# A buffer of its own for the first weight load of each block, paid for with two of four row buffers

## The chip, the cores and the metric

The kernel runs on one core of one Trainium2 chip. The metric is the device time of one execution in microseconds (us). The kernel before has a median of 1816.11 us over three runs (1810.0, 1816.11 and 1819.2).

## The reference

Two layers, each `x <- x + W_out(mixer(rms_norm(x)) * silu(gate))`, on a sequence of 1024 rows and a model width of 1024, with 16 heads of 64. Layer 1 is an attention over all earlier rows with a forget gate. Layer 2, which the change touches, has three groups of dilated windows:

```
qkv = proj[..., :3 * N_GROUPS * INNER].reshape(B, S, 3, N_GROUPS, N_HEADS, HEAD_DIM)
q = apply_partial_rotary(rms_norm(qkv[:, :, 0], q_g[:, None, :]), cos, sin)
k = apply_partial_rotary(rms_norm(qkv[:, :, 1], k_g[:, None, :]), cos, sin)
v = qkv[:, :, 2]
for g, (window, dilation) in enumerate(((128, 1), (512, 4), (2048, 16))):
    o_g, lse_g = dilated_window_attention(q[:, :, g], k[:, :, g], v[:, :, g], window, dilation)
wts = softmax(lses, axis=0)
o = sum over g of wts[g] * o_g
```

So layer 2 needs a projection with 9 x 1024 columns of weights, which is most of its work, then small attention tiles, a weighted sum over the groups, and the output projection.

## The kernel before, in words

**Blocks.** Layer 2 works through 24 blocks, in the list `order`: first group 0 of the eight head pairs, then for each head pair group 2 and group 1. A block projects the eight tiles of 128 rows (t = 0 to 7) by 384 columns of weights (keys, queries and values of two heads). One tile is 24 matmuls at line 313 of `project`: eight slabs of 128 weight rows, three products each, because every operand is split into a high and a low part. All three products of a slab go to one PSUM tile `pj`, of which there are three.

**Weights.** Class `Weights` brings the 384 columns of a block in four loads of two slabs each (`load`, the DMA at L253), into tiles `raw` of which there are two. For the value columns `bound` (L258, VectorE, "vm<-raw") takes a maximum, so a scale can be found later; `split` casts a slab to its high part on ScalarE (L289) and subtracts on GpSimd or, for slabs 4 and 6, on VectorE (L291). The split slabs go to tiles `w`, of which there are 12: eight that the running block multiplies with and four more. So slabs 0 to 3 of the next block can be split at any time in a block, and slabs 4 to 7 only when the last tile of the running block has used its first slabs. A `raw` tile is free again when `bound` and both splits of its two slabs are done.

**Order.** `Flow` counts slots, four to a tile and 32 to a block. `ahead` puts the steps for the next block at slots of the running one: loads at 0, 4, 13 and 20, bounds at 9, 14, 22 and 27, the scale at 28, splits at 10, 11, 15, 16, 29, 29, 30 and 30. These slots fix the order of the program. TensorE keeps that order (`manual_schedule`); for the other engines and for the one DMA queue, SyncE's (SP), the framework's planner makes the order in advance, from its own estimates of durations: what is ready, with a free buffer, goes when the engine is idle, the earlier in the program first. On the chip each engine and the queue then run that fixed order, and wait at the head of it.

**Head norms.** After every second tile `heads_pair` finishes the norms of two tiles: `u` at L378 reads the projection out of PSUM, and L422 scales it by a factor that lies in the same `pj` tile. Until L422 has run, that `pj` tile isn't free. A DMA transpose (L430, "qk_t<-hl") turns queries and keys; `dsw_pair` scores them (L450), and a second DMA transpose (L913, "ptt<-ph") turns the weights for the products with the values (L506 to L508).

**The tag `ga`.** In layer 2 tiles of 2 KB per partition with the tag `ga` are used in two places only. In block 7 (the last of group 0) `reload_x` brings the normed rows again in another column order: two loads per tile t (L983, "x<-xn_d", 16 in all), each followed by a cast on ScalarE (L987) and a subtraction on VectorE (L988) that write over columns of `xh` and `xl` when tile t has been projected. The next block needs these columns: its tile t = 3 reads the last of them. In block 23, the last, `turn_y` brings the finished attention rows of the first seven head pairs (L711, "yt<-y_d"), two loads per tile t of four and three column blocks, which TensorE turns at L346 ("pt<-ident,yt") for the output projection. For a pair of tiles the four loads are asked for at slots 0 to 3 after the second tile and the four turns stand at slots 4 to 7 in TensorE's order. Four tiles with the tag `ga` serve both places.

**Pools.** `lay` takes tiles from a pool of the running layer, with the number of buffers per tag from `CFG`; layer 2's numbers apply from the last tile of the first part of its gate projection on.

Of the kernel before, what the change touches and what calls it, by code (L numbers as in the profile page):

```python
# [51 lines left out]
def tile_cols(g, t):  # L52


    if g < 2:
        return slice(t * P, (t + 1) * P, 1)
    a = 2 * P * (t % 4) + t // 4
    return slice(a, a + 2 * 127 + 1, 2)
# [24 lines left out]
def trunk(ctx, tc, ins, out, cfg):  # L83
# [23 lines left out]
    layer = {}  # L107
# [8 lines left out]
    def lay(shape, dtype, name, tag):  # L116
        return layer["pool"].tile(shape, dtype, name=name, tag=tag, bufs=layer["bufs"][tag])
# [120 lines left out]
    class Weights:  # L238
# [7 lines left out]
                self.vm2 = sm.tile([P, KT // 2], F32R, name="vm2", tag="vm2")  # L246

        def load(self, i, tag=None):
            if tag is None:
                self.raw[i] = w_p.tile([P, 2, 384], F32, name="raw", tag="raw", bufs=2)  # L250
            else:
                self.raw[i] = lay([P, 2, 384], F32, name="raw", tag=tag)
            nc.sync.dma_start(self.raw[i][:, :, : self.n], self.src[:, 2 * i : 2 * i + 2, :])  # L253
# [54 lines left out]
    def project(w, cols):  # L308
        n = w.n
        ps = under["ps"] = ps_pj.tile([P, 512], F32, name="pj", tag="pj")  # L310
        for k in range(KT):
            for i, (a, j) in enumerate(((xh, 0), (xh, 1), (xl, 0))):
                nc.tensor.matmul(ps[:, :n], a[:, k, cols], w.slabs[k][:, j, :n], start=(k == 0 and i == 0), stop=(k == KT - 1 and i == 2))  # L313
            if k % 2:
                flow.tick()
        return ps
# [143 lines left out]
    def v_tile(vs):  # L460
        vt = lay([P, NT, 2, 129], F16, name="vt", tag="vt")
        nc.scalar.activation(vt[:, :, :, 128], vs.unsqueeze(2).broadcast_to([P, NT, 2]), AF.Copy)
        return vt
# [242 lines left out]
    def turn_y(t, g, slots):  # L706
        for h, (n, (s0, s1)) in enumerate(zip((4, 3), slots)):

            def load(h=h, n=n, s1=s1):
                yt = lay([P, 512], F32, name="yt", tag="ga")  # L710
                nc.sync.dma_start(yt[:, : n * P], y_d[tile_rows(g, t), 512 * h : 512 * h + n * P])  # L711

                def go():
                    transpose_rows(yt, 4 * h, n, t)
                    turned.add((t, h))

                flow.at(s1, go)

            flow.at(s0, load)
# [12 lines left out]
    for hp in range(NHP):  # L732
# [8 lines left out]
        vt = v_tile(w.vs)  # L741
        vsr = sm.tile([P, NT], F32, name="vsr", tag="vsr")
        nc.scalar.activation(vsr, rx[:, 0], AF.Copy, scale=w.vs)
        for t in range(NT):
            ps = project(w, tile_cols(0, t))
# [246 lines left out]
    for ci, (hp, g) in enumerate(order):  # L992
        w2 = (dsw_weights(ci + 1) if ci + 1 < len(order) else part(w_do, 0)).ahead()
        vt = v_tile(w.vs)
# [3 lines left out]
        for t in range(NT):  # L998
            if ci == NHP - 1:
                reload_x(t)  # L1000
            ps = project(w, tile_cols(g, t))
# [20 lines left out]
            else:  # L1022
                cmb = {}
# [31 lines left out]
    layer["cm"].__exit__(None, None, None)  # L1055


CFG = dict(pin=1, bc=((1, 0, 26), (1, 1, 28), (0, 0, 38), (0, 1, 46)), wl=(0x50, 0x50), ps=0, pv=100, ph_=100, ph=1, wbufs=12, pl=3, um=3, lpf=8, lsd=((16, 16), (16, 14), (14, 11)), ty2=((0, 4), (1, 5)), hb=1, ub=2, qb=1, nb=3, fox=(((0, 0, 2, 2), (2, 4)), ((0, 0), (4, 4))), due=(29, 33, 39, 45, 35, 41, 49, 57), l1=dict(ga=7, ptt=3, ph=2, p=4, qk_t=6, vt=3, gsl=3), l2=dict(ga=4, cmb=3, ptt=3, ph=2, p=2, qk_t=3, og=3, vt=3, gsl=3, par=1), wload=(0, 4, 13, 20), wbound=(9, 14, 22, 27), wscale=28, wsplit=(10, 11, 15, 16, 29, 29, 30, 30))


def host_layout(inputs):
# [49 lines left out]
```

## Time and profile before

| what | value |
|---|---|
| median of three runs | 1816.11 us |
| the profiled execution's own time | 1818.5 us |
| span of the trace in it | 1816.7 us |
| mean granted TensorE clock | 0.990 |
| busy: TensorE matmul, VectorE, ScalarE, GpSimd | 96%, 60%, 56%, 54% |

Times in a trace count from the first instruction. Busy is the share of the span in which an engine runs an instruction; matmuls overlap, so a busy TensorE is one that has no gap, not one at its peak. Layer 2's blocks lie from about 710 to 1720 us; block 7 from about 1036 to 1081, block 23 from about 1670 on. Then comes the output projection (L336) up to the end. A line of waits reads: engine and line that waited, what it waited for, us in total, times, longest.

### The profile page before, as it was taken

How to read it: one execution, taken by the hardware profiler on the slowest of the kernel's cores; microseconds unless marked ns; L12 is line 12 of the kernel's file. 1: busy time of each engine (PE TensorE's matmuls, PEld its weight loads, DVE VectorE, ACT ScalarE, POOL GpSimd, SP SyncE). 2: the span in 40 equal slices, each digit the busy share in tenths (PEclk: the TensorE clock that was granted, in tenths of full speed). 3: DMA queues.
4: the chain of work that ended last, by engine and by line, in shares of the span. 5: the costliest groups of instructions: out<-in, count | busy, mean ns of one | idle time of the engine just before them, and what ended most of it. 6: DMA issues, size and time to landing. Idle time of an engine off the chain costs nothing.

```text
span 1816.7 us, 38150 instructions
## 1 busy us (share of the span) xinstructions
PE 1737.0 (96%) x13276; PEld 1641.7 (90%) x13276; DVE 1093.3 (60%) x3674; ACT 1011.0 (56%) x2696; POOL 973.5 (54%) x1175
## 2 busy tenths in 40 slices
PE   7999999999988989999999999999999999999999
PEld 6999888888876779999999989999999999999877
DVE  8546666666664453365556585666675666667631
ACT  6536666666665465455555665555555555555620
POOL 4215565556545431255656566667576666757530
PEclk9999999999999999999999999999999999999999
DMA  8447999999999763456767687667677776667852
GB/s 285 127 130 140 193 190 185 176 177 183 187 190 207 213 188 114 127 113 134 142 133 144 146 191 143 157 140 152 138 163 144 162 151 143 149 140 179 189 154 85
DMA packets 653189, 290.79 MB, mean 160 GB/s; under 512 B 512306, under 2 KB 616754, under 8 KB 652996
## 3 DMA queue, kind: packets, MB, share of 16 engines
q1 hardware_dynamic: 652996, 288.36, 71.4%
q8 instruction: 104, 1.70, 0.4%
q14 instruction: 89, 0.73, 0.1%
HBM read 126.46 MB, written 37.03 MB: 90 GB/s over the span
## 4 chain that ended last, share of the span: by engine, by line
PE 45%; DMA 12%; DVE 6%; ACT 4%; issue 3%; POOL 3%; SPq 1%; DVEq 0%; POOLq 0%; ACTq 0%
PE pj L313 33%; PE pj L336 7%; DMA raw<-in_w_dsw 5%; PE s L450 2%; DMA qk_t<-hl 2%; DMA ptt<-ph 2%; DMA og_d<-og 1%; POOL hl L425 1%; POOL w L291 1%; DMA cmb<-og_d 1%; DVE w L291 1%; DVE hl L426 1%; DVE u L422 1%; PE ob L506 1%; DVE p L906 1%
## 5 line engine op out<-in xcount | busy, mean ns | idle before, releaser
L313 PE MATMUL pj<-w,xh 128*128 128x384 f32 (+2 forms) x4864 | 1259.6, 341 | 30.2 <-ACT w L289 7.3
L313 PEld LDWEIGHTS pj<-w,xh 128*128 128x128 f32 x4864 | 873.1, 191 | 38.9 <-DVE ge L481 7.8
L313 PE MATMUL pj<-w,xl 128*128 128x384 f32 (+2 forms) x2432 | 817.6, 336 | 0.2 <-DVE xl L530 0.2
L313 PEld LDWEIGHTS pj<-w,xl 128*128 128x128 f32 x2432 | 464.7, 191 | 0.9 <-DVE xl L530 0.9
L291 POOL TENSOR_TENSOR w<-raw,w 128x384 fp32r<-128x384 f32 (+2 forms) x258 | 261.7, 1035 | 233.3 <-ACT w L289 228.8
L498 POOL TENSOR_TENSOR ph<-p,ph 128x512 f16<-128x512 f32 (+3 forms) x176 | 172.9, 999 | 161.9 <-ACT ph L495 160.7
L289 ACT CAST w<-raw 128x384 fp32r<-128x384 f32 (+2 forms) x352 | 162.6, 501 | 114.8 <-PE pj L336 37.4
L425 POOL TENSOR_TENSOR hl<-u,hl 128x512 f16<-128x512 f32 x128 | 151.2, 1181 | 125.0 <-ACT hl L424 124.9
L912 POOL TENSOR_TENSOR ph<-p,ph 128x768 f16<-128x768 f32 (+2 forms) x96 | 155.3, 1618 | 102.9 <-ACT ph L911 102.9
L383 ACT ACTIVATE sq<-pj 128x256 f32<-128x256 f32 x256 | 97.2, 380 | 168.9 <-DVE u L378 167.2
L450 PE MATMUL s<-qk_t 128*128 128x128 f16 (+1 forms) x1504 | 162.0, 248 | 19.2 <-DVE acc L658 10.4
L336 PE MATMUL pj<-xh,w 128*128 128x512 f32 x512 | 170.4, 404 | 2.2 <-ACT p L907 1.1
L258 DVE TENSOR_REDUCE vm<-raw 128x1 f32<-128x256 f32 x128 | 53.6, 419 | 156.2 <-DMA raw<-in_w_dsw 118.6
L506 PEld LDWEIGHTS <-ptt 128*128 128x128 f16 x1136 | 102.9, 98 | 48.8 <-issue 27.5
L389 DVE SCALAR_TENSOR_TENSOR vt<-pj,vsr,vt 128x128 f16<-128x128 f32 x256 | 89.6, 350 | 93.2 <-ACT vt L388 92.8
L450 PEld LDWEIGHTS <-qk_t 128*128 128x128 f16 x1504 | 110.2, 98 | 36.1 <-issue 22.0
L424 ACT CAST hl<-u 128x512 f16<-128x512 f32 x128 | 79.2, 619 | 104.9 <-DVE u L422 88.6
L495 ACT CAST ph<-p 128x512 f16<-128x512 f32 (+3 forms) x176 | 88.9, 537 | 72.7 <-DMA ptt<-ph 72.3
L492 ACT ACTIVATE p<-p,acc 128x512 f32<-128x512 f32 (+2 forms) x192 | 109.0, 609 | 30.6 <-DVE acc L658 27.4
L336 PEld LDWEIGHTS pj<-xh,w 128*128 128x128 f32 x512 | 97.6, 191 | 24.5 <-DVE xr L779 1.5
L378 DVE TENSOR_TENSOR u<-pj,gr 128x256 f32<-128x256 f32 x256 | 106.4, 416 | 18.4 <-PE pj L313 18.3
L907 ACT ACTIVATE p<-p,og 128x128 f32<-128x128 f32 (+1 forms) x256 | 98.1, 441 | 33.6 <-DVE og L906 33.4
(171 smaller groups left out, 2609.4 us busy)
## 6 DMA issues: line engine op xcount, KB each, us to landing
raw<-in_w_dsw SPq DMA_DIRECT2D x96, 384.0 KB, 3.7
raw<-in_w_fox SPq DMA_DIRECT2D x32, 384.0 KB, 3.7
og_d<-og SPq DMA_DIRECT2D x64, 132.0 KB, 3.2
cmb<-og_d SPq DMA_DIRECT2D x64, 132.0 KB, 3.3
bc<-c_d SPq DMA_DIRECT2D x32, 256.0 KB, 3.9
gs_d<-ge SPq DMA_DIRECT2D x32, 192.0 KB, 3.2
xt<-in_xt SPq DMA_DIRECT2D x16, 256.0 KB, 6.1
xrow<-in_x SPq DMA_DIRECT2D x8, 512.0 KB, 6.3
```

The source lines that it names most:

```text
L289: nc.scalar.copy(w[:, 0, :n], raw[:, k % 2, :n])
L291: eng.tensor_sub(w[:, 1, :n], raw[:, k % 2, :n], w[:, 0, :n].bitcast(F32))
L313: nc.tensor.matmul(ps[:, :n], a[:, k, cols], w.slabs[k][:, j, :n], start=(k == 0 and i == 0), stop=(k == KT - 1 and i == 2))
L336: nc.tensor.matmul(ps[m], w.slabs[k][:, j, m * P : (m + 1) * P], a[:, k, 512 * b : 512 * (b + 1)], start=(k == 0 and x == 0), stop=(k == K ...
L378: nc.vector.tensor_mul(u[:, t % 2].rearrange("p (a b) d -> p a b d", a=2), ps[:, : 4 * HD].rearrange("p (a b d) -> p a b d", a=2, b=2), gr ...
L425: nc.gpsimd.tensor_sub(hl[:, :, :4, 1], u, hl[:, :, :4, 0])
L450: nc.tensor.matmul(s[:, c0 : c0 + cnt * P].rearrange("p (c s) -> p c s", c=cnt), qk[:, i, blk], kk[:, j : j + cnt, e], start=(h == 0), sto ...
L492: nc.scalar.activation(p, p, AF.Exp, bias=acc, scale=-1.0)
L498: (nc.gpsimd if pool_l else nc.vector).tensor_sub(ph[:, e, 1, cols], p, ph[:, e, 0, cols])
L506: nc.tensor.matmul(o[:, e, :], hi, vt[:, j, e, HD:], start=(b == 0), stop=False, skip_group_check=True)
L907: nc.scalar.activation(p[:, e], p[:, e], AF.Exp, bias=acc[:, e : e + 1], scale=-1.0)
L912: nc.gpsimd.tensor_sub(ph[:, 1], st["p"], ph[:, 0])
```

## The change

The first load of each set of weights, whenever layer 2's buffer numbers hold, goes to a tile with the new tag `raw0` (one buffer of 3 KB per partition); loads 1 to 3 share the two `raw` tiles. The tag `ga` has two buffers in layer 2, not four. Layer 1 keeps its numbers.

```diff
         def load(self, i, tag=None):
+            if i == 0 and tag is None and "raw0" in layer["bufs"]:
+
+                tag = "raw0"
             if tag is None:
                 self.raw[i] = w_p.tile([P, 2, 384], F32, name="raw", tag="raw", bufs=2)
             else:
                 self.raw[i] = lay([P, 2, 384], F32, name="raw", tag=tag)
...
-l2=dict(ga=4, cmb=3, ptt=3, ph=2, p=2, qk_t=3, og=3, vt=3, gsl=3, par=1)
+l2=dict(ga=2, cmb=3, ptt=3, ph=2, p=2, qk_t=3, og=3, vt=3, gsl=3, par=1, raw0=1)
```

More of the change, by code (lines that the diff above doesn't have):

```diff
@@ L1055, in trunk @@
     layer["cm"].__exit__(None, None, None)
-CFG = dict(pin=1, bc=((1, 0, 26), (1, 1, 28), (0, 0, 38), (0, 1, 46)), wl=(0x50, 0x50), ps=0, pv=100, ph_=100, ph=1, wbufs=12, pl=3, um=3, lpf=8, lsd=((16, 16), (16, 14), (14, 11)), ty2=((0, 4), (1, 5)), hb=1, ub=2, qb=1, nb=3, fox=(((0, 0, 2, 2), (2, 4)), ((0, 0), (4, 4))), due=(29, 33, 39, 45, 35, 41, 49, 57), l1=dict(ga=7, ptt=3, ph=2, p=4, qk_t=6, vt=3, gsl=3), l2=dict(ga=4, cmb=3, ptt=3, ph=2, p=2, qk_t=3, og=3, vt=3, gsl=3, par=1), wload=(0, 4, 13, 20), wbound=(9, 14, 22, 27), wscale=28, wsplit=(10, 11, 15, 16, 29, 29, 30, 30))
+CFG = dict(pin=1, bc=((1, 0, 26), (1, 1, 28), (0, 0, 38), (0, 1, 46)), wl=(0x50, 0x50), ps=0, pv=100, ph_=100, ph=1, wbufs=12, pl=3, um=3, lpf=8, lsd=((16, 16), (16, 14), (14, 11)), ty2=((0, 4), (1, 5)), hb=1, ub=2, qb=1, nb=3, fox=(((0, 0, 2, 2), (2, 4)), ((0, 0), (4, 4))), due=(29, 33, 39, 45, 35, 41, 49, 57), l1=dict(ga=7, ptt=3, ph=2, p=4, qk_t=6, vt=3, gsl=3), l2=dict(ga=2, cmb=3, ptt=3, ph=2, p=2, qk_t=3, og=3, vt=3, gsl=3, par=1, raw0=1), wload=(0, 4, 13, 20), wbound=(9, 14, 22, 27), wscale=28, wsplit=(10, 11, 15, 16, 29, 29, 30, 30))
 def host_layout(inputs):
```

## The prediction

> **What bounds the kernel now.** I read the page's busy shares first, then the windows of layer 2, then who TensorE and VectorE wait for there, and last the chain of waits around one block.
>
> ```profile
> span 1816.7 us, 38150 instructions
> ...
> PE 1737.0 (96%) x13276; PEld 1641.7 (90%) x13276; DVE 1093.3 (60%) x3674; ACT 1011.0 (56%) x2696; POOL 973.5 (54%) x1175
> ```
>
> ```profile
> 710.00:1040.00 330.00, 328.83 (x2532) 322.66 (x2531) 184.99 (x628) 184.77 (x501) 172.85 (x215) 1.00 0.64 132
> 1040.00:1085.00 45.00, 41.15 (x324) 39.87 (x323) 33.36 (x92) 30.82 (x80) 25.91 (x26) 0.96 0.86 195
> 1085.00:1670.00 585.00, 576.23 (x4305) 562.52 (x4305) 390.66 (x1454) 326.28 (x990) 390.60 (x535) 1.00 0.69 150
> 1670.00:1720.00 50.00, 46.46 (x339) 43.88 (x338) 32.39 (x110) 30.76 (x89) 26.66 (x37) 0.97 0.86 192
> ```
>
> The columns are stretch, length, busy TensorE, weight loads, VectorE, ScalarE, GpSimd, clock, DMA share, GB/s. TensorE is the bound, and in layer 2 it hardly stops: the four stretches leave it idle for 1.17, 3.85, 8.77 and 3.54 us, 17.3 us of 1010. Nothing in this change makes a matmul shorter, so a gain must come out of those 17.3 us and the low clock that follows a gap. The two short stretches, with block 7 and block 23, hold 7.4 us of the idle time in a tenth of the length. They are the two places that use the tag `ga`, and their DMA share is the highest, 0.86. TensorE's own waits over the whole stretch 710 to 1720:
>
> ```profile
> PE pj L313 <- DVE u L422: 6.0, 7, 1.6
> PE pj L313 <- DVE vt L389: 4.8, 4, 2.6
> PE pt L346 <- issue: 2.6, 1, 2.6
> ```
>
> Seven waits for L422 and four for L389: a projection cannot start since VectorE is late to free a `pj` tile. Why VectorE is late, the chain of waits shows in block 15:
>
> ```profile
> 1164.49 4.26 DMA raw<-in_w_dsw
> ...
> 1169.91 0.70 DVE u L422
> ...
> 1170.74 8.75 PE pj L313 x48
> ```
>
> A weight load, then L422 on VectorE, then the matmuls. VectorE stands in its fixed order before a bound (L258) and waits for the load, with L422 behind it. Its timeline at this place, and the sum of these waits in layer 2:
>
> ```profile
> 1167.73 0.42 DVE L258 TENSOR_REDUCE vm<-raw 128x1 f32<-128x256 f32 x1 [1.66 <-DMA raw<-in_w_dsw]
> 1168.77 0.42 DVE L258 TENSOR_REDUCE vm<-raw 128x1 f32<-128x256 f32 x1 [0.62 <-DMA raw<-in_w_dsw]
> ```
>
> ```profile
> DVE vm L258 <- DMA raw<-in_w_dsw: 118.6, 81, 3.5
> ```
>
> VectorE loses 118.6 us to the loads in 81 waits, but only 10.8 us (6.0 + 4.8) of what it is late reaches TensorE.
>
> **Part 1, the first load's own buffer.** It adds and removes no instruction: 96 loads before and after, the same bounds and splits. What moves is the moment at which a load may start. Timelines of GpSimd and of the DMA queue at the same block start:
>
> ```profile
> 1161.27 2.36 POOL L291 TENSOR_TENSOR w<-raw,w 128x384 fp32r<-128x384 f32 x2
> ```
>
> ```profile
> 1164.00 0.89 SPq L253 DMA_DIRECT2D raw<-in_w_dsw  x2
> ```
>
> The last splits of the block that begins end at 1163.63 (1161.27 + 2.36), and the next block's loads 0 and 1 go at 1164.00: they waited for the two `raw` tiles. With a third tile, load 0 needs only that splits 0 and 1 of the block before are done, which happens half a block to a block earlier. But the two `raw` tiles still come free at this moment, and then it is loads 1 and 2 that go into them; the bounds of 1 and 2 then stand where those of 0 and 1 stood, and wait for the same landings. Where load 2 went, after splits 0 and 1, now the load 0 of the block after next can go. So the same four releases start four loads per block, each one place further on. What the loads gain is lead for slabs 0 and 1, and slabs 4 and 5; the latter wait for free `w` tiles, not for data. The gain lies between all of the 10.8 us (if the bounds leave the places where VectorE has no slack) and a loss of 2 us (a bound or a split put ahead of a head pair that is due: one bound of 0.42 us at five of the places). I take a gain of 2 us, near the lower end, by the argument that the releases stay. The gate projection and the output projection use the tile too; I cost that at nothing, since their splits wait for free slabs. If that cover is gone it is one landing, some 4 us by the row above.
>
> **The price of a gap.** Two costs below are gaps of TensorE, and a gap has an aftermath. Block 7 shows it:
>
> ```profile
> 1049.04 0.62 PE L313 MATMUL pj<-w,xh 128*128 128x384 f32 x2 [2.60 <-DVE vt L389]
> ...
> 1050.41 0.84 PE L313 MATMUL pj<-w,xh 128*128 128x384 f32 x2
> ...
> 1053.29 0.53 PE L313 MATMUL pj<-w,xh 128*128 128x384 f32 x2
> ...
> 1053.83 0.51 PE L313 MATMUL pj<-w,xh 128*128 128x384 f32 x2
> ```
>
> From 1050.41 to 1053.29 nine matmuls start, one in 0.32 us; the next three take 0.54 us, 0.18 us each. A gap of 2.6 us therefore costs 9 x 0.14 = 1.3 us on top. The Trainium skill, "TensorE: Matmul & The Clock Gate", Part 1, says that the clock is halved after an idle window of about 3.4 us that runs free of the kernel; by that a gap of 2.6 us would cost nothing more and the sum below would be 1.3 us lower. The trace decides: half the rate after 2.60 us.
>
> **Part 2, two `ga` tiles in block 7.** No instruction is added here either; 16 loads, casts and subtractions remain. The rows: L983's loads, their landing, cast and subtraction, then the queue.
>
> ```profile
> L983 SPq DMA_DIRECT2D x<-xn_d x16: 359/494/855, 693.8 to 1078.1; - x16
> ...
> DMA to landing us min/median/max: 2.9/3.6/4.8
> ```
>
> ```profile
> L988 DVE TENSOR_TENSOR xl<-x,xh 128x512 fp32r<-128x512 f32 x16 | 16.2, 1012 | 1.3 <-ACT xh L987 1.3
> ...
> L987 ACT CAST xh<-x 128x512 fp32r<-128x512 f32 x16 | 9.7, 614 | 0.0
> ```
>
> ```profile
> 1044.91 2.34 DVE L988 TENSOR_TENSOR xl<-x,xh 128x512 fp32r<-128x512 f32 x1
> ...
> 1060.76 0.68 DVE L988 TENSOR_TENSOR xl<-x,xh 128x512 fp32r<-128x512 f32 x1
> ```
>
> ```profile
> 1047.27 0.36 SPq L983 DMA_DIRECT2D x<-xn_d  x1
> ...
> 1065.25 1.07 SPq L983 DMA_DIRECT2D x<-xn_d  x2
> ```
>
> ```profile
> SPq L983 <- DVE u L378: 8.2, 1, 8.2
> ```
>
> The first loads go at 693.8, long before their use: the planner fills every free `ga` tile. With four, two tiles t are ahead; with two, one. From then on each load waits for a subtraction: at 1047.27 at once after the one that ends at 1047.25, but at 1065.25 3.8 us after the one that ends at 1061.44, since the queue was at other work. So a ring of two makes one t per landing, cast, subtraction and queue: 3.6 + 0.6 + 1.0 + (0 to 3.8) = 5.2 to 9.0 us. There are seven steps from 1047.25. The next block reads the last of these columns in its tile t = 3:
>
> ```profile
> 1096.73 0.51 PE L313 MATMUL pj<-w,xh 128*128 128x384 f32 x2
> ```
>
> That leaves (1096.7 - 1047.3) / 7 = 7.1 us a step. At 5.2 nothing is lost; at 8.0 the columns are 7 us late. The added wait is on the DMA queue: 14 loads, not 12, wait at its head, and behind them stand the transposes of L430 and L913 and the weight loads. One such wait was 8.2 us long already. I take 2 us, between 0 and 8; the steps seem nearer to 6 than to 8.
>
> **Part 3, two `ga` tiles in block 23.** TensorE turns four loads per pair of tiles, in its fixed order. First and third of the first two groups of four, then the queue, then the loads' landing:
>
> ```profile
> 1682.66 0.60 PE L346 MATMUL pt<-ident,yt 128*128 128x128 f32 x4
> ...
> 1685.92 0.63 PE L346 MATMUL pt<-ident,yt 128*128 128x128 f32 x4
> ```
>
> ```profile
> 1694.73 0.60 PE L346 MATMUL pt<-ident,yt 128*128 128x128 f32 x4
> ...
> 1698.64 0.60 PE L346 MATMUL pt<-ident,yt 128*128 128x128 f32 x4
> ```
>
> ```profile
> 1684.84 1.23 SPq L913 DMA_TRANSPOSE ptt<-ph  x1
> 1686.17 1.01 SPq L711 DMA_DIRECT2D yt<-y_d  x2
> ...
> 1695.80 1.27 SPq L711 DMA_DIRECT2D yt<-y_d  x2
> ```
>
> ```profile
> yt<-y_d SPq DMA_DIRECT2D x16, 192.0 KB, 3.3
> ```
>
> With four tiles all four loads lie ready. With two, the third load needs the first turn's tile. In the first group that is free at 1683.26; issued at once, the load lands at 1686.6 (+ 3.3), 0.7 us after TensorE wants it at 1685.92; behind the transpose, at 1686.17 as the queue stands now, it lands at 1689.5, 3.6 us late. In the second group it goes at 1695.80 and lands at 1699.1, 0.5 us late. I count nothing for the third group, where TensorE already waits 2.6 us, and 0.5 us for the last. Sum 1.7 to 4.6 us, 6 with one aftermath of 1.3 us; other queue orders can double it. I take 4 us, between 0 (a VectorE that is late anyway hides it) and 10.
>
> **The sum.** -2 + 2 + 4 = +4 us against the profiled execution's 1818.5 us. That one is 2.4 us above the median 1816.11; on the median's base the forecast is 1820 us.
>
> **The rivals.** *Faster:* the bounds do leave the tight places. For it: every one of the seven L422 waits may be a bound's, as in block 15. Against it: the releases that start the loads stay where they are. It gives 1816 - 10.8 - 1.3 = 1804 us if `ga` costs nothing. The Trainium skill, "Perfetto Trace Analysis", Optimization Strategy, says that the same gap repeating on the engine that should be saturated can mean too little SBUF for the next tile. The seven gaps of 6.0 us in all agree with it; that a weight tile is what lacks, no run shows yet.
>
> *Slower:* the ring of two goes round through the queue for each tile, at 8.5 us a step in block 7 (10 us late, 1.3 aftermath) and at 4 us of stall in block 23. It decides from 7.1 us a step on. For it: the 3.8 and 8.2 us that L983 and its queue already waited; against it: 2.9 us as the shortest landing. 1816 + 11 + 4 - 2 = 1829 us.
>
> *It doesn't do what it says:* load 0 stays behind other work in the queue and goes no earlier; then only `ga` counts, 1816 + 6 = 1822 us.
>
> **How the numbers follow.** About 0.5% (9 us) is what a measurement of this kernel can tell from no change. Forecast 0.45; faster 0.14; slower 0.36; no effect of the load 0.05, which falls within 0.5%. So faster by over 0.5% 0.14, within 0.50, slower 0.36. The range is 1806 to 1837 us: it cuts the faster rival's end and the slower one's far end. The forecast's own range, from the bounds that lie nearest to the values taken, is 1812 to 1826.
>
> **What would show it.** Right: one load of each block goes in mid-block, two still go together at a block's start, and L258 waits there as long as before; L346 waits for "yt<-y_d" in block 23. Wrong: the waits for L422 are gone from TensorE's list (faster), or tile t = 3 of block 8 waits for L988, or the windows of blocks 7 and 23 grow by over 5 us each (slower).

## The result, and the profile after

The changed kernel takes 1822.23 us (median of 14 runs) against 1815.76 us for the kernel before (14 runs); the ratio is 1.0038 with a 95% interval of 1.0028 to 1.0048. By the ratio that is a loss of 6.9 us (5.1 to 8.7), below 0.5%; the differences below are worked out from the ratios in the same way. The forecast was 1820 us, +4 us. One execution of the kernels below, of e5, took 2391.7 us at a granted clock of 0.655 and is left out of its time.

By its page, the changed kernel runs as many instructions on each of the five rows of engines as before, and TensorE is busy for 4.7 us less, so the loss is idle time. All its line numbers from L249 on are three higher (L253 is L256, L422 is L425, L450 is L453).

```profile
span 1821.2 us, 38060 instructions
...
PE 1732.3 (95%) x13276; PEld 1636.8 (90%) x13276; DVE 1087.7 (60%) x3674; ACT 1011.5 (56%) x2696; POOL 977.8 (54%) x1175
```

Where the time went shows when both profiles are cut at the same work. I cut where the scale's small matmul (L270, L273 after) starts in the last tile of some blocks: before block 0, block 7, block 8 and block 9, and before block 23. The windows of the kernel before, then of the changed one (stretch, length, busy TensorE, weight loads, VectorE, ScalarE, GpSimd, clock, DMA share, GB/s):

```profile
0.00:755.10 755.10, 697.62 (x5628) 643.76 (x5629) 440.29 (x1357) 444.24 (x1046) 343.06 (x345) 0.98 0.78 177
755.10:1030.40 275.30, 274.13 (x2141) 268.15 (x2140) 159.64 (x567) 157.23 (x436) 160.28 (x200) 1.00 0.68 137
1030.40:1076.40 46.00, 42.15 (x329) 40.87 (x329) 34.12 (x98) 29.30 (x76) 27.14 (x30) 0.96 0.82 179
1076.40:1116.90 40.50, 40.40 (x329) 39.44 (x329) 26.92 (x93) 27.11 (x76) 25.46 (x30) 1.00 0.75 161
1116.90:1663.60 546.70, 538.03 (x3998) 525.24 (x3998) 365.05 (x1365) 302.75 (x925) 365.78 (x504) 1.00 0.69 151
1663.60:1816.70 153.10, 144.63 (x860) 124.26 (x858) 67.26 (x197) 50.38 (x141) 51.77 (x66) 0.99 0.56 144
```

```profile
0.00:752.10 752.10, 693.92 (x5628) 639.15 (x5629) 440.52 (x1358) 443.48 (x1046) 345.50 (x345) 0.99 0.78 178
752.10:1025.60 273.50, 272.97 (x2141) 267.87 (x2140) 159.16 (x570) 158.70 (x439) 162.42 (x201) 1.00 0.68 139
1025.60:1069.90 44.30, 41.15 (x330) 39.39 (x329) 32.12 (x84) 27.19 (x69) 25.11 (x30) 1.00 0.74 176
1069.90:1115.10 45.20, 40.39 (x330) 39.44 (x328) 27.81 (x106) 28.56 (x79) 26.73 (x32) 1.00 0.85 161
1115.10:1664.60 549.50, 537.40 (x3998) 525.12 (x3997) 361.75 (x1363) 302.95 (x923) 366.07 (x503) 1.00 0.68 149
1664.60:1821.20 156.60, 146.41 (x860) 125.87 (x858) 66.31 (x197) 50.63 (x141) 52.00 (x66) 0.97 0.54 141
```

Read the lengths, row against row. The first stretch is layer 1 and, from about 660 us on, layer 2's gate projection; block 0 starts at about 759 us, not at the 710 us given above. This stretch is 3.0 us shorter, which can't be told from chance: the profiled runs of the kernels below spread over 750.3 to 756.5 us there, and e1 and e10, which have no tile of their own either, take 751 us. Then come -1.8 us (blocks 0 to 6), -1.7 us (block 7), +4.7 us (block 8), +2.8 us (blocks 9 to 22) and +3.5 us (block 23 and the output projection). So the change wins before its first cost and loses in three places. TensorE's waits in layer 2 (710 to 1725 us) have changed their names:

```profile
PE s L453 <- DMA qk_t<-hl: 14.0, 9, 2.6
PE pj L316 <- DVE vt L392: 3.7, 6, 1.1
PE pj L316 <- DVE u L425: 2.8, 3, 1.2
PE pt L349 <- DMA yt<-y_d: 2.7, 1, 2.7
PE pt L349 <- DVE xl L354: 2.3, 1, 2.3
```

The waits for VectorE's L422 and L389 fell from 10.8 to 6.5 us, which is the kind of gain that the early load was to bring. The waits of the scores for the transposed queries and keys, 2.4 us in the same list of before, are now 14.0 us.

**Block 23.** TensorE's timeline, and the DMA queue's, at the first group of four turns:

```profile
1689.74 0.94 PE L349 MATMUL pt<-ident,yt 128*128 128x128 f32 x4 [2.66 <-DMA yt<-y_d]
...
1692.40 0.84 PE L349 MATMUL pt<-ident,yt 128*128 128x128 f32 x3
```

```profile
1684.83 1.52 SPq L916 DMA_TRANSPOSE ptt<-ph  x1
1686.44 1.00 SPq L714 DMA_DIRECT2D yt<-y_d  x2
```

The third load went behind the transpose, at 1686.44, and TensorE stood 2.66 us for it. The turns after the gap take 0.94 and 0.84 us, against 0.60 and 0.49 us in the rows of before: the aftermath.

**Blocks 7 and 8.** ScalarE's waits between 1025 and 1090 us, TensorE's scores in block 8, and the queue:

```profile
ACT xh L990 <- DMA x<-xn_d: 10.1, 8, 1.9
```

```profile
1077.31 1.06 PE L453 MATMUL s<-qk_t 128*128 128x128 f16 x12 [2.23 <-DMA qk_t<-hl]
...
1090.02 1.06 PE L453 MATMUL s<-qk_t 128*128 128x128 f16 x12 [2.57 <-DMA qk_t<-hl]
```

```profile
1038.64 0.38 SPq L986 DMA_DIRECT2D x<-xn_d  x1
...
1068.75 0.53 SPq L986 DMA_DIRECT2D x<-xn_d  x1
...
1070.32 0.41 SPq L986 DMA_DIRECT2D x<-xn_d  x1
1071.32 3.09 SPq L433 DMA_TRANSPOSE qk_t<-hl  x1
1074.51 2.63 SPq L986 DMA_DIRECT2D x<-xn_d  x2
```

With two tiles ScalarE waits for eight of the x loads, 10.1 us, a wait that the same list of before doesn't have, and the transposes come late among them in the queue. The loads of the first half tile go at 1038.6 for t = 1 and at 1074.5 for t = 7, six steps later: 6.0 us a step. The columns themselves are not late for tile t = 3 of block 8: no wait of TensorE is for L991, the subtraction that writes them. What is late is the work behind the loads.

**A pair block.** One of the new waits, in block 10, in the chain of waits (the place that the prediction calls block 15 is the start of this same block 10):

```profile
1165.75 1.00 POOL w L294
...
1167.16 0.96 POOL w L294
...
1168.15 3.21 DMA raw<-in_w_dsw
...
1171.38 0.42 DVE vm L261
...
1172.43 1.90 DVE hl L429
...
1174.39 4.49 DMA qk_t<-hl
...
1178.93 0.83 PE s L453 x8
```

GpSimd's splits, the block's fourth load behind them, its bound, and only then VectorE's copy of `hl` and the transpose that TensorE waits for. The queue's timeline shows the loads:

```profile
1160.73 0.39 SPq L256 DMA_DIRECT2D raw<-in_w_dsw  x1
...
1161.71 0.42 SPq L256 DMA_DIRECT2D raw<-in_w_dsw  x1
...
1164.00 0.33 SPq L256 DMA_DIRECT2D raw<-in_w_dsw  x1
...
1168.15 0.33 SPq L256 DMA_DIRECT2D raw<-in_w_dsw  x1
```

Three loads now go within 3.3 us at the block's start, where before two went at 1164.00 and two at 1171.11. Slabs 0 and 1 of the next block lie in their own tile already, so their splits can run as soon as slab tiles come free. By the order of the program, the load at 1164.00 is already load 0 of the block after next, and the one at 1168.15 waits for the splits of slabs 2 and 3, the two in the chain.

### The profile page after: what moved, and what is told of

It reads as the page before. It is cut to its first block, busy times and chain, and to the rows that moved or that the text cites. A ratio compares the mean times of both kernels' runs of the same rounds, so it can differ in the third digit from the quotient of the medians.

```text
span 1821.2 us, 38060 instructions
## 1 busy us (share of the span) xinstructions
PE 1732.3 (95%) x13276; PEld 1636.8 (90%) x13276; DVE 1087.7 (60%) x3674; ACT 1011.5 (56%) x2696; POOL 977.8 (54%) x1175
## 4 chain that ended last, share of the span: by engine, by line
PE 41%; DMA 13%; POOL 6%; DVE 5%; ACT 4%; issue 3%; SPq 1%; DVEq 0%; POOLq 0%; ACTq 0%
PE pj L316 31%; PE pj L339 6%; DMA raw<-in_w_dsw 3%; POOL w L294 3%; DMA qk_t<-hl 2%; PE s L453 2%; DMA ptt<-ph 1%; DMA og_d<-og 1%; POOL hl L428 1%; DMA yt<-y_d 1%; DMA cmb<-og_d 1%; DVE u L425 1%; POOL cmb L942 1%; ACT w L292 1%; PE ob L509 1%
## 5 line engine op out<-in xcount | busy, mean ns | idle before, releaser
L294 POOL TENSOR_TENSOR w<-raw,w 128x384 fp32r<-128x384 f32 (+2 forms) x258 | 268.7, 1057 | 214.8 <-ACT w L292 211.9
L428 POOL TENSOR_TENSOR hl<-u,hl 128x512 f16<-128x512 f32 x128 | 150.2, 1173 | 125.6 <-ACT hl L427 125.3
L915 POOL TENSOR_TENSOR ph<-p,ph 128x768 f16<-128x768 f32 (+2 forms) x96 | 155.8, 1623 | 111.6 <-ACT ph L914 108.6
L453 PE MATMUL s<-qk_t 128*128 128x128 f16 (+1 forms) x1504 | 160.3, 246 | 30.4 <-DMA qk_t<-hl 15.2
L453 PEld LDWEIGHTS <-qk_t 128*128 128x128 f16 x1504 | 109.5, 98 | 47.4 <-issue 21.9
L392 DVE SCALAR_TENSOR_TENSOR vt<-pj,vsr,vt 128x128 f16<-128x128 f32 x256 | 89.5, 350 | 93.6 <-ACT vt L391 92.6
L261 DVE TENSOR_REDUCE vm<-raw 128x1 f32<-128x256 f32 x128 | 53.5, 418 | 143.6 <-DMA raw<-in_w_dsw 104.6
L429 DVE COPY hl<-hl 128x512 f16<-128x512 f16 x128 | 69.1, 540 | 89.0 <-POOL hl L428 88.8
```

What stands on the lines that cost most here:

```text
L294: eng.tensor_sub(w[:, 1, :n], raw[:, k % 2, :n], w[:, 0, :n].bitcast(F32))
L428: nc.gpsimd.tensor_sub(hl[:, :, :4, 1], u, hl[:, :, :4, 0])
L453: nc.tensor.matmul(s[:, c0 : c0 + cnt * P].rearrange("p (c s) -> p c s", c=cnt), qk[:, i, blk], kk[:, j : j + cnt, e], start=(h == 0), sto ...
L915: nc.gpsimd.tensor_sub(ph[:, 1], st["p"], ph[:, 0])
```

## The experiments

Every time below is compared with the kernel before on the same chip. Theory A says that the two rings of two are the loss; its rival B, that the early load itself does the harm.

**e1: the rings of two alone.** The kernel before with one number changed:

```diff
-l2=dict(ga=4,
+l2=dict(ga=2,
```

> The kernel before with two ga tiles in layer 2 and no raw0. Theory A (the loss is the two-tile ring, in blocks 7 and 8 and in block 23; the first load's own tile is worth within 2 us of nothing): 6 to 9 us slower than before, about as slow as the changed kernel or slower; TensorE waits for the transposes of L430 in block 8 and for yt in block 23. Theory B (the early load itself does the harm, since splits 0 and 1 move to the start of a block and delay GpSimd's part of the head norms): within 3 us of before.

1825.44 us, ratio 1.0050 (1.0036 to 1.0064): 9.1 us slower than before. A holds and B alone falls. The interval overlaps that of the changed kernel, so the tile of its own is worth nothing that these runs tell from zero (some 2 us) on top of the rings. The expected waits were not there under those names: TensorE waited for VectorE in block 8 (L389, 4.0 us) and for VectorE's L351 at the turns of block 23 (5.7 us).

**e2: block 7's ring relieved.** The tiles of the tag `cmb` lie idle until block 9:

```diff
-            xt = lay([P, 4, P], F32, name="x2", tag="ga")
+            xt = lay([P, 4, P], F32, name="x2", tag=("ga", "cmb")[h])
```

> The changed kernel, but reload_x takes every second tile from the tag cmb, which no block up to block 8 uses, so block 7 has two ga tiles and three cmb tiles. Theory A: 3 to 5 us faster than the changed kernel; the two gaps of TensorE in block 8 that end with a transpose of L433 (2.4 and 2.7 us) and ScalarE's waits for x are gone. Theory B: no change against the changed kernel.

1819.0 us, ratio 1.0010 (0.9996 to 1.0023), against 1.0038 (1.0028 to 1.0048) for the change: 5 us better, and the intervals don't meet. The windows of blocks 7 and 8:

```profile
1024.20:1065.50 41.30, 40.88 (x330) 39.60 (x329) 33.44 (x87) 27.27 (x72) 24.99 (x27) 1.00 0.82 190
1065.50:1108.40 42.90, 40.82 (x325) 39.81 (x324) 28.73 (x102) 27.56 (x77) 27.41 (x34) 0.96 0.86 156
```

84.2 us against 89.5 us (44.3 + 45.2), and less than the 86.5 us of before. ScalarE no longer waits for an x load. Of the two gaps in block 8 the second is gone; the first stays, at 2.08 us. Here the expectation was wrong: that gap is not the ring's. Block 8 is the first pair block, and the gap goes with the tile of its own there: it is in the traces of e4 (1.71 us) and e6 (1.99 us) below, and in none of e1, e5 and e7, where the pair blocks have no such tile.

**e3: the turns of a pair further apart.**

```diff
-[(flow.now + a + 2 * i, flow.now + b + 2 * i) for a, b in cfg["ty2"]]
+[(flow.now + a + 2 * i, flow.now + b + 4 * i) for a, b in cfg["ty2"]]
```

> The changed kernel, but in block 23 the turns of the second tile of each pair stand four slots after those of the first, not two, so a load with two ga tiles has some 5 us from the turn that frees its tile to its own turn. Theory A: 2 to 4 us faster than the changed kernel; TensorE's gap before L349 for yt (2.7 us) is gone. Theory B: no change.

1819.41 us, ratio 1.0011 (0.9997 to 1.0025): 5 us better than the change. Its turns, in TensorE's timeline:

```profile
1681.36 0.60 PE L349 MATMUL pt<-ident,yt 128*128 128x128 f32 x4
...
1687.25 0.61 PE L349 MATMUL pt<-ident,yt 128*128 128x128 f32 x4
...
1717.14 0.63 PE L349 MATMUL pt<-ident,yt 128*128 128x128 f32 x4 [2.22 <-DMA yt<-y_d]
```

The first group runs without a gap, its third turn 5.9 us after the first. One gap of 2.22 us for yt stays in the last group, so the cure is partial. Block 23 and the output projection take 152.1 us in its profile, against 156.6 us in that of the change.

**e4: both.** The two edits together.

> The changed kernel with both edits: x tiles from ga and cmb, and the turns four slots apart. The early load stays, and both places of the two-tile ring are relieved. Theory A: 1814 to 1817 us, level with before. Theory B: 1820 us or more.

1814.77 us, ratio 0.9991 (0.9978 to 1.0005): no loss left. Within the noise the two mends add up, and the two rings account for the loss. But there is no gain either, so the question became where the early load's gain goes. Theory A1 for the next kernels: it gains in group 0 and loses in the pair blocks. A2: it does nothing anywhere.

**e5 and e6: the tile of its own in one part of the layer only.** To e4, with `g == 0` in e5 and `g != 0` in e6:

```diff
-        def __init__(self, src, n, vcols=None, layer=0):
+        def __init__(self, src, n, vcols=None, layer=0, own=False):
...
-            self.raw, self.slabs, self.vs = {}, [], None
+            self.raw, self.slabs, self.vs, self.own = {}, [], None, own
...
-            if i == 0 and tag is None and "raw0" in layer["bufs"]:
+            if i == 0 and tag is None and "raw0" in layer["bufs"] and self.own:
...
-        return Weights(w_dsw[g, hp], 384, slice(256, 384), 1)
+        return Weights(w_dsw[g, hp], 384, slice(256, 384), 1, g == 0)
```

> The kernel of e4, but only the blocks of group 0 load to raw0; the pair blocks (groups 2 and 1) and the weights of the gate and output projections use the two raw tiles for all four loads. Theory A1 (the tile of its own pays in group 0, some 5 to 7 us, up to the block that reloads x, and costs as much in the pair blocks, where it lets splits 0 and 1 of GpSimd go ahead of the head norms and the transposes of L433 go late): 1807 to 1811 us; TensorE's waits at L453 for qk_t fall from 11.8 us to under 5 us. Theory A2 (the tile is worth nothing anywhere; the profiles' differences by block are chance): 1813 to 1817 us.

> The kernel of e4, but only the pair blocks load to raw0. Theory A1: 1817 to 1822 us, the waits at L453 for qk_t stay near 11 us and the waits for L425 and L392 in block 7 are back. Theory A2: 1813 to 1817 us.

e5: 1812.42 us, ratio 0.9974 (0.9959 to 0.9990), a little above the 1807 to 1811 us that A1 expected. e6: 1821.78 us, ratio 1.0027 (1.0009 to 1.0044). The intervals lie on both sides of 1, so A2 falls. TensorE's wait for the transposes, in e5 (expected: under 5 us) and then in e6 (expected: near 11 us):

```profile
PE s L453 <- DMA qk_t<-hl: 3.1, 2, 2.8
```

```profile
PE s L453 <- DMA qk_t<-hl: 8.4, 6, 2.2
```

**e7: the mends without the tile.** e4 without `raw0=1`.

> The kernel of e4 without raw0: two ga tiles with the x tiles from ga and cmb and the turns four slots apart. Against e4 it prices the whole tile of its own with the rings relieved. Theory A1: within 3 us of e4, with L425 and L392 as TensorE's waits in place of L453. If the tile of its own were a gain hidden by the rings, this kernel would be 5 us slower than e4.

1816.27 us, ratio 1.0000 (0.9984 to 1.0016). Against it the tile gains 4.7 us in group 0 (1.0000 - 0.9974), loses 4.9 us in the pair blocks (1.0027 - 1.0000), and both together come to -1.6 us (e4, where the gate and output projections use the tile too), which the intervals can't tell from zero. The interval of e7 just overlaps with that of e5 and with that of e6, so each of the two sizes is uncertain by some 4 us; that e5 and e6 differ is clear. The profiles, one execution each, put the loss where A1 has it: blocks 8 to 22 take 591.9 us in e6 and 585.8 us in e7. For the gain in group 0 they are less clear: blocks 0 to 7 are 1.7 us shorter in e5 than in e7, and 4.9 us shorter in e4 than in e6. Which wait the tile removes there was not traced.

**e8: the early splits off GpSimd.** e4, with bits 0 and 1 of layer 2's mask set, so that slabs 0 and 1 are subtracted on VectorE as slabs 4 and 6 are:

```diff
-wl=(0x50, 0x50)
+wl=(0x50, 0x53)
```

> The kernel of e4 with the subtractions of slabs 0 and 1 in layer 2's blocks on VectorE, not GpSimd, so that what the early load lets go ahead is off GpSimd. Theory G (GpSimd's early splits delay the low part of the head norms, L428, and so the transposes): the waits at L453 fall to under 6 us and VectorE's waits for L428 from 72 to about 60 us; the time is 1809 to 1814 us unless VectorE's 25 us more work makes up for it. Theory Q (the loads take places in the DMA queue ahead of the transposes): the waits at L453 stay near 11 us.

1805.19 us (six runs), ratio 0.9934 (0.9913 to 0.9954): 12 us below before, the fastest of all, and below the 1809 to 1814 us that G expected. TensorE's waits in blocks 9 to 22, in e4 (1108.4 to 1659.5 us) and then in e8 (1110.6 to 1650.8 us):

```profile
PE s L453 <- DMA qk_t<-hl: 8.7, 5, 2.4
PE pj L316 <- DVE u L425: 2.1, 4, 0.6
PE pj L316 <- DVE vt L392: 2.0, 3, 0.7
```

```profile
PE pj L316 <- DVE u L425: 4.2, 6, 1.4
```

VectorE's waits for GpSimd's part of the head norms in all of layer 2, in e4 and then in e8:

```profile
DVE hl L429 <- POOL hl L428: 71.9, 46, 5.1
```

```profile
DVE hl L429 <- POOL hl L428: 58.1, 49, 2.1
```

This sum is 68.6 to 72.4 us in the change, e2, e3 and e6, and 54.4 to 61.2 us in all the other kernels. Theory G said under 6 us and about 60 us; Q, which has the loads in the transposes' way, said 11 us. In all of layer 2 the waits at L453 are 4.0 us, of which 2.9 us are the first gap of block 8. They are gone from blocks 9 to 22, although three loads still go together in block 10, within 2.0 us (1156.96 to 1158.92), so Q falls.

**e9, e10, e11: the controls.** The same edit on the kernel before (e9), on e7 (e10) and on the changed kernel (e11).

> The kernel before, untouched but for the subtractions of slabs 0 and 1 in layer 2's blocks, which go to VectorE. A control for e8. Theory G (only with the early load do these subtractions stand ahead of the head norms): within 4 us of before. Theory H (GpSimd was too full in layer 2 in any case, and e8's gain of 10 us against e4 has nothing to do with the early load): 1806 to 1809 us, 8 to 10 us faster than before.

> The kernel of e8 without raw0 (that of e7 with the two subtractions on VectorE). It prices the tile of its own once GpSimd is relieved. Theory G: 1812 to 1817 us, as e7, so the tile is worth 8 to 11 us there. Theory H: 1805 to 1808 us, as e8, so the tile is worth nothing.

> The changed kernel, with its rings of two unrelieved, but the subtractions of slabs 0 and 1 on VectorE. Theory G and the sum of the earlier runs: e8's 1805 us plus the 7 us that the rings cost, 1810 to 1814 us; TensorE's waits at L453 fall from 14.0 us to about 7 us, those of block 8 staying.

e9: 1820.78 us, 1.0024 (1.0010 to 1.0037). e10: 1819.8 us, 1.0015 (1.0000 to 1.0031). e11: 1812.0 us, 0.9980 (0.9967 to 0.9993). So the edit by itself costs some 4 us on the kernel before and 3 us on e7; G had said within 4 us and 1812 to 1817 us, so it is a little dearer than expected, and H falls. With it, the tile of its own takes the mended kernel from 1.0015 to 0.9934, 15 us where G had 8 to 11, and it turns the change itself into a gain of 3.6 us with both rings still at two. e11's waits at L453 are 4.8 us (expected: about 7), with none in blocks 9 to 22. Without the tile the edit puts VectorE in trouble, as e9's waits of TensorE show; e8's rows above have no such wait, and VectorE waits 72.5 us for the loads there (L261), against 100.1 us in e10.

```profile
PE pj L313 <- DVE vt L389: 11.7, 7, 3.4
```

How the early splits reach the transposes, the order on VectorE shows. In block 10 and every second block after it, the changed kernel, e4 and e6 run the bound of the last load, and the product of the maxima behind it (L263), ahead of the copy of `hl`. The kernel before, e5, e7, e8 and e11 run the copy first there. Block 10 of e8, in VectorE's timeline:

```profile
1166.63 0.47 DVE L429 COPY hl<-hl 128x512 f16<-128x512 f16 x1
...
1167.70 0.42 DVE L261 TENSOR_REDUCE vm<-raw 128x1 f32<-128x256 f32 x1 [0.59 <-DMA raw<-in_w_dsw]
```

In all five waits for a transpose in blocks 9 to 22 of the changed kernel, GpSimd's part of the norms (L428) had ended 1.1 to 2.9 us before the copy started. So it isn't L428 that comes last there, as Theory G has it, but VectorE's work ahead of the copy; in four of the five, either L263 or the copy itself takes 1.45 to 1.97 us. What stays open is by which of its estimates the planner turns that order round. Every edit lets it order the whole layer anew; that the two-by-two of tile and edit (e7, e4, e10, e8) has its gain in one corner only speaks for the mechanism and against chance.

## Why the prediction was right

**The bound.** Right: TensorE is the bound, no matmul got shorter, and all of the difference is in its gaps.

**Part 1, the tile of its own.** The net value was right, -2 us taken and some -2 us measured (e1 against the change, e4 against e7; neither clear of zero), but by luck: within the noise it is the sum of two larger terms that I didn't see, 4.7 us gained in group 0 and 4.9 us lost in the pair blocks. The step that failed is that two of the loads still go together at a block's start and one goes in mid-block: three go together, since the splits of slabs 0 and 1, with their data there, move to the block's start as well. I had bounded a loss at 2 us, counting a bound of 0.42 us at five places. A bound ahead of a head pair that is due is indeed what the traces show, but with up to 1.97 us for VectorE's work behind it, and a transpose of over 4 us after that; the price hangs, by e8, on whether GpSimd has the two early subtractions of 1 us each. VectorE's waits for the bounds fell from 118.6 to 102.2 us, not far from the "as long as before" of the prediction.

**Part 2, block 7.** The ring was taken at 2 us between 0 and 8. Its step, 6.0 us, is what I thought nearest, below the 7.1 us at which the columns would be late, and they are not late. It cost 5 us all the same (e2 against the change). The term was mis-sized because its bounds came from the lateness of the columns; the waits went to what I had named without a price, the transposes queued among the loads, and to ScalarE, whose waits I had not named at all.

**Part 3, block 23.** 4 us taken; 3.5 us in the profile, 5 us by e3. The place, the transpose ahead of the load and the aftermath are as written. In all, a term too small by 3 us and a net of -2 us that hid two others make the forecast of +4 us fall within 3 us of the measured 6.9 us.

**The rivals.** Slower by over 0.5% didn't happen: the step stayed at 6.0 us, under the 7.1 us from which that rival was to decide. The faster rival's 1804 us is what e8 reaches at 1805 us, with the early splits off GpSimd and the rings relieved, but only in part by its mechanism: the waits for L389 are gone from blocks 9 to 22, while those for L422 are 4.2 us there, against 6.0 us before. The Trainium skill's rule on repeating gaps, "Perfetto Trace Analysis", Optimization Strategy, was half right here: a weight tile was lacking, in that e8 is 15 us faster than e10, but giving the tile alone (e4 against e7) brought nothing clear of noise.

## What to carry to other kernels

A buffer taken from a ring can cost more than the lateness of its data: each load then waits at the head of an in-order queue, so price what stands behind it and the engine that consumes it. An earlier load lets a greedy planner pull forward the steps that hung on it; ask on which engine these steps land and what they then stand ahead of, there and on the engines behind. When such a change measures as nothing, try it in one half of the program and then in the other: here the parts were -4.7 and +4.9 us.

## What the runs showed of the hardware

**VectorE beside GpSimd.** Between 1085 and 1670 us of the changed kernel, VectorE's copy of `hl`, 128 x 512 in 16 bits, takes from 0.28 to 1.97 us. Of the 61 copies, 24 take 0.71 us or more, and all of these lie beside an instruction of GpSimd; of the 35 that take under 0.35 us, 33 don't overlap with one by more than 0.1 us. The longest is the one in the chain of block 10, beside GpSimd's subtraction of `ph`, in the timelines of the two engines:

```profile
1172.36 1.97 DVE L429 COPY hl<-hl 128x512 f16<-128x512 f16 x1
```

```profile
1172.51 1.67 POOL L915 TENSOR_TENSOR ph<-p,ph 128x768 f16<-128x768 f32 x1
```

The copy ends at 1174.33, right after GpSimd's 1174.18. The Trainium skill, "SBUF — State Buffer", Who interferes with whom, says that a VectorE instruction in a mode that uses two ports contends with GpSimd for a shared pair of ports, and that whoever issues first blocks the other for the whole instruction. The trace agrees that VectorE is held up for the length of GpSimd's instruction, with 1.97 us for a copy whose median is 0.30 us in this stretch. Whether the copy ran in that mode no run shows, nor who issued first: another instruction of GpSimd (L939, 1172.34 to 1172.55) was under way when the copy started. L263, on 128 x 4 numbers, does the same: it takes 1.45, 1.53 and 1.66 us before three of the five waits, each time ending with GpSimd's L915, and 0.16 us at its shortest.

**The clock after a gap.** The gap of 2.60 us in block 7 of the kernel before is followed by a granted clock of 0.50 from 1051.0 to 1053.3 us, and the one of 2.08 us in block 8 of e2 by 0.56 from 1076.0 to 1078.0. But in block 8 of the changed kernel the granted clock is 1.00 after gaps of 2.23 and 2.57 us, and the scores behind both take 1.06 us, against 1.51 us in e2. So a gap of this length has an aftermath in some cases and none in others, and the 1.3 us of the prediction is its price only where it comes.
